# First blocks of the v products: one column piece over two token tiles in place of two pieces over one, with the second tile's rows of x loaded early

## The chip, the cores and the metric

The kernel runs on one core of one Trainium2 chip. The metric is the device time in microseconds of one execution, median of the runs; lower is better. A profiled execution of the kernel, with the start, the length and the waits of each instruction, was taken beside the timed ones.

## What is computed

One step of a two-layer streaming encoder for 1024 prompt rows and 32 sample rows of width 1024 that share all weights. The part that the change touches lies in the first layer:

```python
mod = jax.nn.silu(c) @ w_ada[i] + b_ada[i]
sh1, sc1, gt1, sh2, sc2, gt2 = jnp.split(mod[:, None, :], N_MOD, axis=-1)
h = rmsnorm(x, g_norm[i, 0]) * (1 + sc1) + sh1
...
z = jax.nn.gelu(h @ w_in)
u, v = jnp.split(z, 2, axis=-1)
v = rmsnorm(v, g_v)
vr = v.reshape(bsz, L // T, T, SGU_GROUPS, SGU_GROUP_DIM)
w = w_s[:, :T, :T] * sgu_chunk_mask()[:T, :T].astype(w_s.dtype)
s = jnp.einsum('gij,bnjgd->bnigd', w, vr)
...
return (u * s) @ w_out, v
```

Behind it come a squared-ReLU MLP of width 4096, a second layer with a pooling mixer, and another such MLP. They make up most of the time and are not changed.

## The kernel before

**Tiles and blocks.** The 1056 rows lie in three token tiles of 384, 384 and 288 rows (the last one: 256 prompt rows and the 32 sample rows). For the loads of x and for the v products the rows are cut into nine blocks: 0 to 2 are tile 0, 3 to 5 tile 1, 6 to 8 tile 2, where block 8 has 32 rows. v has 2048 columns, in four column pieces `p` of 512. A product `(p, b)` is the block's 128 rows by the piece's 512 columns, over eight steps `k` of 128 of the inner width. As every fp32 operand is split into a high and a low part (`wh`, `wl` for weights; `hh`, `hl` for activations), each step is three matmuls (`v_mm`, L815 to L832): 24 for a whole product. For block 8 it is two to a step.

**The stream.** All weights and the rows of x are read by DMAs that one list, `stream`, orders (L304 to L337); `issue` (L349) walks along it and starts each load as soon as its buffer allows. There are two kinds of buffer: a ring of three `raw` tiles of 4 KB a partition, used for x, for weights of the products and for the later slices of `w_ada`; and the 16 `W` tiles, which hold the first 16 slices of `w_ada` (those ahead of `first_ada`) and all split weights. All loads are issued by SyncE's queue (SPq), in order, and SPq also issues the stores of v (`v_end`, L844).

**What becomes of an item.** `stream_step` (L541) takes the next item. `do_w` (L369) splits a weight: a copy on ScalarE into `wh` (L372), a subtraction on VectorE into `wl`. `do_x` (L497) squares and sums a block on ScalarE (L502), turns it with eight transposes on TensorE (L512) into two PSUM tiles, which VectorE copies into `acc` (L515). `do_ada_pe` (L394) multiplies an early `w_ada` slice on TensorE (L404); two slices make 256 modulation columns, ScalarE copies them out (L416), TensorE turns them (L421), VectorE folds them (L423) into `mod` and `coef`. Later slices go through VectorE alone (`do_ada`, into `aa`), with a small fold on TensorE (L458).

**The first norm.** `first_norm(t)` (L789) is a generator: `spread` makes the reciprocal roots of a tile's rows (L621 to L641), ending with the small products `pb_h` on TensorE and a copy (L794); then each of eight `next` runs one step k of `apply` (L760): `mt` on VectorE, `hh` on ScalarE (L777), `hl` on VectorE. `h0`, `h1`, `h2` are the three tiles' generators. `hh[t]` and `hl[t]` live in rooms `h` and `l` of tile t, each of 8 x 384 words a partition for tiles 0 and 1.

**The early part** (L857 to L885). Five products run while the modulation still arrives: `(0,0)`, `(0,1)`, `(0,2)`, `(1,0)`, `(1,1)`, all of tile 0, the first three in the PSUM tiles `pd`, the other two in `pu`. Four quarters q follow one another; in each, weight items `v,0,q` and `v,1,q` come in, two steps of `h0` are applied, the next four `w_ada` slices are folded, and each of the five products runs its steps 2q and 2q+1. In quarter 2 the blocks 3 to 5 of x come in and the statistics of tile 1 are made, in quarter 3 the blocks 6 to 8 and those of tile 2. After the last quarter the rest of `h1` and all of `h2` are applied and the five products end (`v_end`: gelu L842, square and sum L843, store L844).

**The order behind it.** `v_order` (L911) lists the remaining products: `(1,2)`, then blocks 3 to 8 of piece 0 and of piece 1, then pieces 2 and 3. After each, `weave` (L612) takes at most one item of the stream. A planner decides whether a later slice of `w_ada` may be taken: it sums its own costs of TensorE (`tick`) and VectorE (`on_dve`) and holds a slice back while VectorE is ahead; the folds of these slices get due times from the same sums. The whole program is then handed to a list scheduler, which fixes for each engine an order of instructions; at run time every engine goes through its list in that order.

Of the kernel before, what the change touches and what calls it, by code (L numbers as in the profile page):

```python
# [16 lines left out]
D = 1024  # L17
# [17 lines left out]
def tile_stream_encoder_step(  # L35
# [33 lines left out]
    def tick(us):  # L69
        time["pe"] += us  # L70
        time["dve"] = max(time["dve"], time["pe"] - 4.0)
# [59 lines left out]
    def room(part, t, name, dtype=F32):  # L131
        return work.tile([P, KB, ncol[t]], dtype, tag=f"h{part}{t}", bufs=1, name=name)
# [13 lines left out]
    def t_c(name):  # L146
        return work.tile([P, 384], F32, tag="c", bufs=3, name=name)
# [7 lines left out]
    def t_raw(name):  # L155
        return work.tile([P, 1024], F32, tag="raw", bufs=RAW_SLOTS, name=name)
# [13 lines left out]
    for i, parts in enumerate(rows):  # L170
        n = sum(k for _, k in parts)
# [11 lines left out]
        v = const.tile([P, n], F32, name=f"vec{i}")  # L183
# [24 lines left out]
    stream = []  # L208
    witem = {}

    def add_w(key, ap, shape):
        stream.append(("w", key, ap, shape))

    def add_ada(l, j):

        sl, q = j // 2, j % 2
        stream.append(
            (
                "ada",
                (l, sl, q),  # L220
                w_ada[l][q * 512 : (q + 1) * 512, sl * 256 : (sl + 1) * 256].rearrange(
                    "(k p) f -> p k f", p=P
                ),
                (4, 256),
            )
        )

    def add_x(b):
        if b < 8:
            ap = x_prompt[0, b * P : (b + 1) * P, :]  # L230
        else:
            ap = x_sample[0]
        stream.append(("x", b, ap, None))

    def v_item(p, q):
        return (
            ("v", p, q),
            sgu_w_in[0][q * 256 : (q + 1) * 256, SGU + p * 512 : SGU + (p + 1) * 512].rearrange(
                "(k p) f -> p k f", p=P
            ),  # L240
            (2, 512),
        )

    def w_vpiece(p):
        for q in range(4):
            add_w(*v_item(p, q))
# [53 lines left out]
    def some_ada(n):  # L300
        for _ in range(min(n, len(rest))):
            add_ada(*rest.pop(0))
# [1 line left out]
    for b in range(3):  # L304
        add_x(b)
    for q in range(4):
        if q == 3:
            for b in range(3, 6):
                add_x(b)
        for j in (8 + 2 * q, 9 + 2 * q, 2 * q, 2 * q + 1):  # L310
            add_ada(0, j)
        for p in range(2):
            add_w(*v_item(p, q))
    first_ada = len(stream)
    for b in range(6, 9):
        add_x(b)
    rest += [(0, j) for j in range(16, 48)]
    some_ada(10)
    for p in range(2, 4):
# [24 lines left out]
    deferred = []  # L344

    def in_raw(k):
        return not (stream[k][0] == "ada" and k < first_ada)

    def issue():  # L349
        while state["issued"] < len(stream):  # L350
            k = state["issued"]
            kind, key, ap, shape = stream[k]
            if in_raw(k):
                if state["raw"] == RAW_SLOTS:
                    return
                state["raw"] += 1
                r = t_raw(f"raw{k}")
            else:
                r = work.tile([P, 1024], F32, tag="W", bufs=W_SLOTS, name=f"raw{k}")
            if kind == "x":  # L360
                nr = P if key < 8 else DEC
                i = nc.sync.dma_start(r[:nr, :], ap)
            else:
                i = nc.sync.dma_start(r.rearrange("p (a b) -> p a b", a=shape[0]), ap)
            raws[k] = r
            loads[key] = i.ins
            state["issued"] += 1
# [122 lines left out]
    def run_deferred(force=False):  # L490
        n = len(deferred)
        while n > 0 and (force or deferred[0][0] <= time["pe"]):
            deferred.pop(0)[1]()
            n -= 1
# [61 lines left out]
    def need_w(key):  # L556
        state["used"] = max(state["used"], wpos[key])
        while key not in witem:
            assert stream_ready(), key
            stream_step()  # L560
        return witem[key]
# [9 lines left out]
    def w_finish(key):  # L571
        wdone.add(key)
# [50 lines left out]
    def spread(t, ss, tag, out, dg):  # L623

        npr, nsm = TILES[t][1], TILES[t][2]
        blk = [(c * P, P) for c in range(npr // P)] + ([(npr, nsm)] if nsm else [])
        nb = len(blk)
        ms, r0, q = t_st(f"ms_{tag}"), t_st(f"r0_{tag}"), t_st(f"q_{tag}")
        ts(ms[:, :nb], ss[:, :nb], 1.0 / D, EPS, op0=ALU.mult, op1=ALU.add)
        act(out=r0[:, :nb], in_=ms[:, :nb], func=AF.Sqrt)  # L630
        nc.vector.reciprocal(out=r0[:, :nb], in_=r0[:, :nb])
        tt(out=q[:, :nb], in0=r0[:, :nb], in1=r0[:, :nb], op=ALU.mult)
        stt(out=q[:, :nb], in0=q[:, :nb], scalar=-0.5, in1=ms[:, :nb], op0=ALU.mult, op1=ALU.mult)
        stt(out=r0[:, :nb], in0=q[:, :nb], scalar=1.5, in1=r0[:, :nb], op0=ALU.add, op1=ALU.mult)
        yield False
        pb = ps_ms(f"pb_{tag}")
        for b, (c0, w) in enumerate(blk):
            act(out=dg[:w, c0 : c0 + w], in_=ident[:w, :w], func=AF.Copy, scale=r0[:w, b : b + 1])
        for b, (c0, w) in enumerate(blk):
            mm(pb[:, c0 : c0 + w], ones[:w, :], dg[:w, c0 : c0 + w], start=True, stop=True)  # L640
        out.append(pb)  # L641
        yield False
# [145 lines left out]
    def first_norm(t):  # L788
        n = ncol[t]  # L789
        nb = 3  # L790
        cp = t_c(f"r_h0_{t}")
        got = []
        yield from spread(t, ssx[:, 3 * t : 3 * t + nb], f"h0_{t}", got, cp)
        act(out=cp[:, :n], in_=got[0][:, :n], func=AF.Copy)  # L794
        yield "statistics"
        yield from apply(t, 0, 0, 0, cp, keep=True)
# [14 lines left out]
    def v_mm(ps, p, b, ks):  # L811
        if b < 8:
            t, c0, m = min(b // 3, 2), (b - 3 * min(b // 3, 2)) * P, P
        else:
            t, c0, m = 2, 256, DEC  # L815
        for k in ks:
            wh, wl = need_w(("v", p, k // 2))
            o = (k % 2) * 512
            if b == 8:
                a = hs[k // 4][:, k % 4, :]  # L820
                tick(0.46)
                mm(ps[: 2 * m, :], a, wh[:, o : o + 512], start=k == 0, stop=False)
                mm(ps[: 2 * m, :], a, wl[:, o : o + 512], start=False, stop=k == KB - 1)
                if k % 2 == 1:
                    w_finish(("v", p, k // 2))
                continue
            tick(0.69)
            a_h = hh[t][:, k, c0 : c0 + m]
            a_l = hl[t][:, k, c0 : c0 + m]
            mm(ps[:m, :], a_h, wh[:, o : o + 512], start=k == 0, stop=False)  # L830
            mm(ps[:m, :], a_h, wl[:, o : o + 512], start=False, stop=False)  # L831
            mm(ps[:m, :], a_l, wh[:, o : o + 512], start=False, stop=k == KB - 1)  # L832
# [13 lines left out]
    def statistics(h):  # L846
        while next(h) != "statistics":
            pass

    def stream_to(kind, key):  # L850
        k = max(i for i, s in enumerate(stream) if s[0] == kind and s[1] == key)
        while state["next"] <= k:
            stream_step()
        run_deferred()


    early = [(0, 0), (0, 1), (0, 2), (1, 0), (1, 1)]  # L857
    early_ps = [(ps_dn if i < 3 else ps_up)(f"pv{p}_{b}") for i, (p, b) in enumerate(early)]
    h0, h1, h2 = (first_norm(t) for t in range(NT))
    stream_to("x", 2)  # L860
    statistics(h0)
    stream_to("ada", (0, 0, 1))
    for q in range(4):
        stream_to("w", ("v", 0, q))
        next(h0)
        stream_to("w", ("v", 1, q))
        next(h0)
        if q < 2:
            stream_to("ada", (0, q + 1, 1))
        elif q == 2:  # L870
            stream_to("x", 5)
            statistics(h1)
            stream_to("ada", (0, 3, 1))
        else:
            stream_to("x", 8)
            statistics(h2)
        for ps, (p, b) in zip(early_ps, early):
            v_mm(ps, p, b, (2 * q, 2 * q + 1))
    for h in (h0, h1):
        for _ in h:  # L880
            pass
    for ps, (p, b) in zip(early_ps, early):
        v_end(ps, p, b)
    for _ in h2:
# [3 lines left out]
    for half in range(2):  # L888
        x = work.tile([P, 384], F32R, tag="rr", bufs=2, name=f"hs{half}")[:, : 8 * DEC].rearrange(
            "p (k n) -> p k n", k=4  # L890
        )
# [16 lines left out]
        stt(out=q, in0=q, scalar=-0.5, in1=m, op0=ALU.mult, op1=ALU.mult)  # L908
        stt(out=x, in0=q, scalar=1.5, in1=x, op0=ALU.add, op1=ALU.mult)

    v_order = [(1, 2)]  # L911
    v_order += [(p, b) for p in range(2) for b in range(3, 9)]
    v_order += [(p, b) for p in range(2, 4) for b in range(9)]
    for p, b in v_order:
        ps = ps_dn(f"pv{p}_{b}")
# [581 lines left out]
```

## Time and profile before

| | us |
|---|---|
| median of 3 runs | 2222.41 (2219.92 to 2223.79) |
| profiled execution, its own time | 2220.61 |
| its span in the trace | 2218.8 |
| TensorE busy in the span | 2187.9 |
| VectorE busy | 1404.1 |
| ScalarE busy | 986.4 |
| mean granted TensorE clock | 0.997 |

Engines are PE (TensorE matmuls), PEld (its weight loads), DVE (VectorE), ACT (ScalarE), POOL (GpSimd) and SP (SyncE); SPq is the DMA issue of SyncE. In a view by instructions in order of time, a row has the start, the duration, the engine and line, the tiles written and read, the count, and in brackets the idle time of the engine before it with what ended it. Matmuls are pipelined: a row's duration is longer than the distance to the next start, and it is the distance that counts. The stretch that the change touches is the first 140 us or so.

### The profile page before, as it was taken

What the parts mean: (1) busy time and instruction counts of PE and PEld (TensorE: products, weight loads), DVE (VectorE), ACT (ScalarE), POOL (GpSimd) and SP (SyncE); (2) the same over time, 40 slices, a digit from 0 to 9 for tenths busy, and PEclk for the clock granted to TensorE, in tenths of its full rate; (3) what the DMA queues carried; (4) which work ended last, traced back from release to release, by engine and by line L of the source; (5) the groups of instructions that cost most, each with busy time, mean ns of one, the idle gap of its engine ahead of it and who ended that gap; (6) DMA issues with size and microseconds to landing.
All of it is one profiled execution on the core that took longest, in us unless ns stands there. A gap on an engine that the chain in (4) does not pass through costs nothing.

```text
span 2218.8 us, 33828 instructions
## 1 busy us (share of the span) xinstructions
PE 2187.9 (99%) x13488; PEld 2096.6 (94%) x13488; DVE 1404.1 (63%) x2646; ACT 986.4 (44%) x1675; POOL 0.7 (0%) x6
## 2 busy tenths in 40 slices
PE   7999999999999999999999999999999999999998
PEld 5777899999999999999999999999999999999998
DVE  4755656665869646676757869878765454433375
ACT  4633423133447553223445556666564542313354
POOL 0000000000000000000000000000000000000000
PEclk9999999999999999999999999999999999999999
DMA  8365533244436543334554556665454552312243
GB/s 299 123 199 196 176 112 126 78 148 126 135 98 194 162 143 124 114 109 125 154 170 140 165 162 187 184 190 155 147 162 140 153 154 64 96 29 77 92 124 110
DMA packets 369090, 312.99 MB, mean 141 GB/s; under 512 B 10818, under 2 KB 345098, under 8 KB 368932
## 3 DMA queue, kind: packets, MB, share of 16 engines
q1 hardware_dynamic: 368660, 310.74, 45.1%
q8 instruction: 105, 1.72, 0.3%
q14 instruction: 53, 0.43, 0.1%
q10 hardware_dynamic: 272, 0.10, 0.0%
HBM read 278.95 MB, written 31.84 MB: 140 GB/s over the span
## 4 chain that ended last, share of the span: by engine, by line
PE 92%; DVE 3%; DMA 3%; ACT 1%; issue 0%; SPq 0%; DVEq 0%; ACTq 0%
PE pf L803 11%; PE pf L804 11%; PE pf L805 11%; PE pg L803 11%; PE pg L804 11%; PE pg L805 11%; PE po L803 3%; PE po L804 3%; PE po L805 3%; PE pu L803 3%; PE pu L805 3%; PE pu L804 3%; PE pv L830 2%; PE pv L831 2%; PE pv L832 2%; DVE aa L79 2%
## 5 line engine op out<-in xcount | busy, mean ns | idle before, releaser
L803 PE MATMUL pg<-fh,wh_dn 128*128 128x384 f32 (+1 forms) x1536 | 499.2, 325 | 0.0
L803 PE MATMUL pf<-hh,wh_up 128*128 128x384 f32 (+1 forms) x1536 | 497.6, 324 | 0.6 <-ACT wh_up L372 0.6
L805 PE MATMUL pf<-hh,wl_up 128*128 128x384 f32 (+1 forms) x1536 | 495.8, 323 | 0.6 <-DVE wl_up L79 0.6
L804 PE MATMUL pf<-hl,wh_up 128*128 128x384 f32 (+1 forms) x1536 | 496.3, 323 | 0.0
L804 PE MATMUL pg<-fl,wh_dn 128*128 128x384 f32 (+1 forms) x1536 | 494.4, 322 | 0.0
L805 PE MATMUL pg<-fh,wl_dn 128*128 128x384 f32 (+1 forms) x1536 | 494.1, 322 | 0.0
L79 DVE TENSOR_TENSOR wl_up<-raw,wh_up 128x1024 fp32r<-128x1024 f32 x152 | 185.8, 1223 | 169.8 <-ACT wh_up L372 169.8
L803 PEld LDWEIGHTS pg<-fh,wh_dn 128*128 128x128 f32 x1536 | 288.5, 188 | 4.0 <-issue 2.4
L803 PEld LDWEIGHTS pf<-hh,wh_up 128*128 128x128 f32 x1536 | 288.2, 188 | 2.8 <-issue 1.4
L804 PEld LDWEIGHTS pg<-fl,wh_dn 128*128 128x128 f32 x1536 | 288.6, 188 | 0.7
L805 PEld LDWEIGHTS pf<-hh,wl_up 128*128 128x128 f32 x1536 | 288.2, 188 | 1.0 <-DVE wl_up L79 1.0
L805 PEld LDWEIGHTS pg<-fh,wl_dn 128*128 128x128 f32 x1536 | 288.6, 188 | 0.0
L804 PEld LDWEIGHTS pf<-hl,wh_up 128*128 128x128 f32 x1536 | 288.2, 188 | 0.4
L372 ACT ACTIVATE wh_up<-raw 128x1024 fp32r<-128x1024 f32 x152 | 161.0, 1059 | 281.5 <-PE pf L804 208.1
L79 DVE TENSOR_TENSOR acc<-acc,pg 128x384 f32<-128x384 f32 (+1 forms) x336 | 173.4, 518 | 141.1 <-PE pg L805 140.5
L372 ACT ACTIVATE wh_dn<-raw 128x1024 fp32r<-128x1024 f32 x152 | 161.0, 1060 | 210.6 <-PE pg L804 164.3
L79 DVE TENSOR_TENSOR wl_dn<-raw,wh_dn 128x1024 fp32r<-128x1024 f32 x152 | 185.9, 1223 | 89.3 <-ACT wh_dn L372 89.0
L79 DVE SCALAR_TENSOR_TENSOR aa<-raw,csil,aa 128x256 f32<-128x256 f32 x560 | 231.2, 478 | 1.8 <-DMA raw<-in_w_ada_dram 1.8
L1121 ACT ACTIVATE r<-pf 128x384 f32<-128x384 f32 (+1 forms) x192 | 86.6, 451 | 202.7 <-PE pf L805 199.3
L79 DVE TENSOR_TENSOR fl<-r,fh 128x384 fp32r<-128x384 f32 (+1 forms) x192 | 100.3, 522 | 105.1 <-ACT fh L957 103.5
L803 PE MATMUL pu<-hh,wh_u 128*128 128x384 f32 (+1 forms) x384 | 126.1, 328 | 0.0
L805 PE MATMUL pu<-hh,wl_u 128*128 128x384 f32 (+1 forms) x384 | 124.4, 324 | 0.8 <-DVE wl_u L79 0.8
(253 smaller groups left out, 2923.7 us busy)
## 6 DMA issues: line engine op xcount, KB each, us to landing
raw<-in_ffn_w_up_dram SPq DMA_DIRECT2D x152, 512.0 KB, 4.1
raw<-in_ffn_w_down_dram SPq DMA_DIRECT2D x152, 512.0 KB, 3.4
raw<-in_w_ada_dram SPq DMA_DIRECT2D x96, 512.0 KB, 4.2
raw<-in_sgu_w_in_dram SPq DMA_DIRECT2D x40, 512.0 KB, 4.1
xd<-acc SPq DMA_DIRECT2D x8, 1536.0 KB, 6.9
raw<-in_sgu_w_out_dram SPq DMA_DIRECT2D x24, 512.0 KB, 3.7
xo_r<-xd SPq DMA_DIRECT2D x32, 384.0 KB, 3.5
vd<-vt SPq DMA_DIRECT2D x32, 256.0 KB, 2.4
```

The source lines that it names most:

```text
L79: return op(out, *args, **kw)
L372: act(out=wh, in_=r, func=AF.Copy)
L803: mm(ps[:, :n], wh, rh, start=i == 0, stop=False)
L804: mm(ps[:, :n], wh, rl, start=False, stop=False)
L805: mm(ps[:, :n], wl, rh, start=False, stop=i == last)
L830: mm(ps[:m, :], a_h, wh[:, o : o + 512], start=k == 0, stop=False)
L831: mm(ps[:m, :], a_h, wl[:, o : o + 512], start=False, stop=False)
L832: mm(ps[:m, :], a_l, wh[:, o : o + 512], start=False, stop=k == KB - 1)
L1121: act(out=r[:, :n], in_=ps[:, :n], func=AF.Relu)
```

## The change

Three things are changed.

- The order of the stream. In each quarter only the item of piece 0 comes in; the four items of piece 1 follow as one run after blocks 6 to 8 of x. Blocks 3 to 5 of x move from quarter 3 of the stream to just behind the first weight item.
- The place of blocks 3 to 5 of x. They are read into the room that `hh[1]` uses afterwards (three blocks of 1024 words fill its 8 x 384 words), and no longer into the ring of three.
- The products of the early part and their order. The five are now blocks 0 to 4 of piece 0; blocks 3 and 4 are of tile 1, so two steps of `h1` are applied in each quarter, after the quarter's products of blocks 0 to 2 and before those of blocks 3 and 4. Blocks 3 to 5 come in and tile 1's statistics are made in quarter 0. Behind the early part the order is `(0,5)`, `(1,0)` to `(1,5)`, then blocks 6 to 8 of both pieces, then pieces 2 and 3 as before.

```diff
     for b in range(3):
         add_x(b)
     for q in range(4):
-        if q == 3:
+        for j in (8 + 2 * q, 9 + 2 * q, 2 * q, 2 * q + 1):
+            add_ada(0, j)
+        add_w(*v_item(0, q))
+        if q == 0:
             for b in range(3, 6):
                 add_x(b)
-        for j in (8 + 2 * q, 9 + 2 * q, 2 * q, 2 * q + 1):
-            add_ada(0, j)
-        for p in range(2):
-            add_w(*v_item(p, q))
     first_ada = len(stream)
     for b in range(6, 9):
         add_x(b)
+    w_vpiece(1)
...
     def in_raw(k):
-        return not (stream[k][0] == "ada" and k < first_ada)
+        return stream[k][1] not in (3, 4, 5) and not (stream[k][0] == "ada" and k < first_ada)
+
+
+    x_rows = room("h", 1, "x_rows").rearrange("p k n -> p (k n)").rearrange("p (b d) -> p b d", d=D)
...
+            elif kind == "x":
+                r = x_rows[:, key - 3, :]
...
-    early = [(0, 0), (0, 1), (0, 2), (1, 0), (1, 1)]
+
+    early = [(0, b) for b in range(5)]
     early_ps = [(ps_dn if i < 3 else ps_up)(f"pv{p}_{b}") for i, (p, b) in enumerate(early)]
     h0, h1, h2 = (first_norm(t) for t in range(NT))
+
+    def early_mm(bs, q):
+        for b in bs:
+            v_mm(early_ps[b], 0, b, (2 * q, 2 * q + 1))
+
     stream_to("x", 2)
     statistics(h0)
     stream_to("ada", (0, 0, 1))
     for q in range(4):
         stream_to("w", ("v", 0, q))
         next(h0)
-        stream_to("w", ("v", 1, q))
         next(h0)
-        if q < 2:
-            stream_to("ada", (0, q + 1, 1))
-        elif q == 2:
+        early_mm((0, 1, 2), q)
+        if q == 0:
             stream_to("x", 5)
             statistics(h1)
-            stream_to("ada", (0, 3, 1))
+        if q < 3:
+            stream_to("ada", (0, q + 1, 1))
         else:
             stream_to("x", 8)
             statistics(h2)
-        for ps, (p, b) in zip(early_ps, early):
-            v_mm(ps, p, b, (2 * q, 2 * q + 1))
-    for h in (h0, h1):
-        for _ in h:
-            pass
+        next(h1)
+        next(h1)
+        early_mm((3, 4), q)
     for ps, (p, b) in zip(early_ps, early):
         v_end(ps, p, b)
...
-    v_order = [(1, 2)]
-    v_order += [(p, b) for p in range(2) for b in range(3, 9)]
+    v_order = [(0, 5)]
+    v_order += [(1, b) for b in range(6)] + [(p, b) for p in range(2) for b in range(6, 9)]
     v_order += [(p, b) for p in range(2, 4) for b in range(9)]
```

## The prediction

> **What bounds the kernel now.** I read the page's first part, then the busy times by stretch, then TensorE's groups and its instructions in order of time for the stretch that the change touches, last the queue of SyncE and the groups of VectorE and ScalarE.
>
> ```profile
> span 2218.8 us, 33828 instructions
> PE 2187.9 (99%) x13488; PEld 2096.6 (94%) x13488; DVE 1404.1 (63%) x2646; ACT 986.4 (44%) x1675; POOL 0.7 (0%) x6
> ```
>
> TensorE is busy nearly throughout; 2218.8 - 2187.9 = 30.9 us are all that it idles, so an edit that adds and removes no matmul can save no more than a part of that. The change ends before 141 us, so the next view splits the first 154 us at the first v product, at the end of the five early ones, and at the start of piece 2. Columns: stretch, its length, PE, PEld, DVE and ACT busy with instruction counts, POOL, granted clock, DMA share, GB/s.
>
> ```profile
> 16.00:24.20 8.20, 6.85 (x58) 2.92 (x58) 2.62 (x9) 3.63 (x9) 0.00 (x0) 0.79 1.03 339
> 24.20:69.60 45.40, 43.42 (x266) 30.66 (x266) 31.50 (x73) 26.77 (x47) 0.00 (x0) 1.00 0.77 258
> 69.60:141.00 71.40, 71.31 (x334) 55.12 (x335) 42.19 (x117) 31.90 (x78) 0.00 (x0) 1.00 0.35 116
> 141.00:154.20 13.20, 10.19 (x41) 6.60 (x39) 8.25 (x16) 5.10 (x7) 0.00 (x0) 0.87 0.72 234
> ```
>
> The early part shows 45.40 - 43.42 = 2.0 us of idle TensorE, the stretch behind it 0.1 us. But busy is not peak, so I work out what the early part's instructions need back to back. Their groups, and the rows from which the distances between starts come (two rows of 128 x 512 products with 31 starts between them, a run of 16 modulation products, a run of 16 transposes, each with the row that follows it):
>
> ```profile
> L830 PE MATMUL pv<-wh_v,hh 128*128 128x512 f32 x40 | 16.2, 417 | 0.1
> L831 PE MATMUL pv<-wl_v,hh 128*128 128x512 f32 x40 | 16.1, 403 | 0.0
> L832 PE MATMUL pv<-wh_v,hl 128*128 128x512 f32 x40 | 15.9, 398 | 0.0
> L404 PE MATMUL ada<-raw,csil 128*32 128x256 f32 x80 | 6.6, 388 | 1.6 <-DMA raw<-in_w_ada_dram 1.6
> L512 PE MATMUL xT<-ident,raw 128*128 128x128 f32 x40 | 5.2, 274 | 0.0
> L421 PE MATMUL adat<-ident,adas 128*128 128x128 f32 x12 | 2.3, 276 | 0.0
> L640 PE MATMUL pb_h<-r_h,ones 128*128 128x128 f32 x6 | 1.3, 320 | 0.0
> L512 PE MATMUL xT<-ident,raw 32*128 32x32 f32 x8 | 0.7, 224 | 0.0
> ```
>
> ```profile
> 23.08 1.07 PE L404 MATMUL ada<-raw,csil 128*32 128x256 f32 x16
> 24.26 0.96 PE L830 MATMUL pv<-wh_v,hh 128*128 128x512 f32 x3
> ...
> 45.37 2.04 PE L512 MATMUL xT<-ident,raw 128*128 128x128 f32 x16
> 47.16 0.48 PE L830 MATMUL pv<-wh_v,hh 128*128 128x512 f32 x1
> ...
> 55.55 1.07 PE L404 MATMUL ada<-raw,csil 128*32 128x256 f32 x16
> 56.55 0.50 PE L830 MATMUL pv<-wh_v,hh 128*128 128x512 f32 x1
> ...
> 69.69 0.50 PE L830 MATMUL pv<-wh_v,hh 128*128 128x512 f32 x1 [0.42 <-ACT pv L843]
> ...
> 73.56 0.39 PE L830 MATMUL pv<-wh_v,hh 128*128 128x512 f32 x1
> ...
> 80.66 0.39 PE L831 MATMUL pv<-wl_v,hh 128*128 128x512 f32 x1
> ```
>
> A product matmul takes (80.66 - 73.56)/31 = 0.229 us, a modulation product 1.00/16 = 0.063, a transpose 1.79/16 = 0.112. So: 120 x 0.229 = 27.5, 80 x 0.063 = 5.0, 40 x 0.112 = 4.5, and for the last small groups at most their busy 2.3 + 1.3 + 0.7 = 4.3: 41.3 us of 45.4. The early part is **bound by TensorE** with 4 us of holes, 2.0 us of them named: 1.6 for modulation slices still in transit, and 0.42 at 69.69, where `(1,2)` waits for the PSUM tile of `(0,0)`.
>
> **The change part by part.** Nothing is computed more or less often: 36 v products, 16 early slices, nine blocks of x and 16 splits remain. What moves is when.
>
> *Transit of the slices (-1.6).* The rows of SPq show why the slices of quarter 2 were late:
>
> ```profile
> 15.59 9.66 SPq L364 DMA_DIRECT2D raw<-in_sgu_w_in_dram  x2
> 25.31 2.29 SPq L364 DMA_DIRECT2D raw<-in_w_ada_dram  x4
> ```
>
> The second of these weight loads stands at the queue's head for most of 9.66 us until a ring tile comes free, and the four slices queue behind it until 25.31. In the new order the item of piece 1 is gone and blocks 3 to 5 need no ring tile, so up to the third weight item SPq waits only for tiles that x held. Twenty transfers stand up to the end of quarter 2's slices (x 6, slices 12, weights 2); at 524 KB and the 339 GB/s of the stretch before 24.2 each takes 1.55 us, so the last lands at about 32 us, before TensorE, with blocks 3 to 5 and ten more products ahead of it, asks. The wait goes whole. 2 MB less travel ahead of quarter 3; that part was already hidden.
>
> *End of the first three products (-0.4).* Blocks 0 to 2 finish twelve matmuls (2.7 us) ahead of 3 and 4, so their gelus can run before `(0,5)` needs a tile.
>
> *Transposes of blocks 3 to 5 (-1.0).* 24 x 0.112 = 2.7 us leave the bound stretch, if they fit ahead of 24.26, where TensorE does 6.85 of 8.20 us at a granted clock of 0.79; the 16 modulation products at 23.08 (1.07) fall behind in exchange, as their slices now land three transfers later. Bounds: -1.6 (all fit) and 0 (none). I take -1.0, since the data of block 3 can land only after seven transfers and one weight item, about 8 x 1.55 + 2 = 14 us, which leaves most of the stretch.
>
> *What blocks 3 to 5 add ahead of the first products (+0.5).* ScalarE gets three squares, VectorE six copies, ahead of or between tile 0's steps:
>
> ```profile
> L515 DVE COPY acc<-xT 128x512 f32<-128x512 f32 x6 | 3.8, 685 | 3.1 <-PE xT L512 3.1
> L79 DVE TENSOR_TENSOR wl_v<-raw,wh_v 128x1024 fp32r<-128x1024 f32 x8 | 9.7, 1223 | 0.7 <-ACT wh_v L372 0.6
> L79 DVE SCALAR_TENSOR_TENSOR mt<-acc,coef,r_h 128x384 f32<-128x384 f32 x8 | 4.7, 616 | 0.1
> L79 DVE SCALAR_TENSOR_TENSOR hl<-mt,mod,hh 128x384 fp32r<-128x384 f32 x6 | 3.4, 613 | 0.7 <-ACT hh L777 0.7
> ```
>
> VectorE is busy 2.62 of 8.20 us before 24.2, so there is room; only a copy standing in its order ahead of tile 0's first `mt` costs. Bounds 0 and 2.0 (three copies); I take 0.5.
>
> *Tile 1's steps inside the quarters (+0.2).* Two steps are 2 x (616 + 613) = 2.5 us of VectorE. A quarter then has 2.5 + 2.5 + 1.2 for one split and about 1 for the folds: 7.2 us, beside at least 30 x 0.229 + 32 x 0.063 = 8.9 us of TensorE; it keeps up. In quarter 0 the copies and the statistics come on top (3.8 + 1), 12 us beside 8.9 + 2.7: TensorE may stand for tile 1's `hh` before blocks 3 and 4. Bounds 0 and 1.5; in its queue the products of blocks 0 to 2 stand ahead, so 0.2. The rest of `h1`, 16 x 0.61 = 10 us, leaves the time after the early part.
>
> *Piece 1's splits (+0.5).* Before, they were done during the quarters. Now `(0,5)`, 24 x 0.229 = 5.5 us, is all that covers them, at about 67.5 to 73 us, and they share VectorE and ScalarE with the steps of tile 2 and the ends of five products:
>
> ```profile
> L79 DVE SCALAR_TENSOR_TENSOR aa<-raw,csil,aa 128x256 f32<-128x256 f32 x14 | 6.1, 475 | 0.0
> L79 DVE SCALAR_TENSOR_TENSOR hl<-mt,mod,hh 128x256 fp32r<-128x256 f32 x8 | 3.8, 480 | 0.3 <-ACT hh L777 0.3
> L79 DVE SCALAR_TENSOR_TENSOR mt<-acc,coef,r_h 128x256 f32<-128x256 f32 x8 | 3.8, 479 | 0.0
> L79 DVE SCALAR_TENSOR_TENSOR mt<-acc,coef,r_h 128x32 f32<-128x32 f32 x8 | 2.0, 247 | 0.0
> L79 DVE SCALAR_TENSOR_TENSOR hl<-mt,mod,hh 128x32 fp32r<-128x32 f32 x8 | 2.0, 247 | 0.1
> ...
> raw<-in_sgu_w_in_dram SPq DMA_DIRECT2D x40, 512.0 KB, 4.1
> ```
>
> Tile 2's steps are 3.8 + 3.8 + 2.0 + 2.0 = 11.6 us of VectorE, the four splits 4 x 1.22 = 4.9. In this same stretch the 14 `aa` instructions (6.1 us), later in the program than those steps, ran between them; the splits can do so as well, and the 10 us of tile 1's steps are gone. Bounds: 0, and 7.5 us if every step of tile 2 goes first (rival 2). Nearest to the `aa` row, I take 0.5.
>
> *Behind it (0).* By the planner's own sums both versions reach the same state after the twelfth product behind the early part, and the folds of the later slices follow the 6th, 8th, 10th and 12th in both. The hole at the start of piece 2 (13.20 - 10.19 = 3.0 us) therefore moves along.
>
> **Sum:** -1.6 - 0.4 - 1.0 + 0.5 + 0.2 + 0.5 = -1.8 us. The profiled execution took 2220.61 (1.8 around its span); it becomes 2218.8. The median lies 1.8 us above it: **2220.6**.
>
> A wait put in newly may cost more than its length:
>
> ```profile
> 144.05 0.48 PE L458 MATMUL ada<-aa,pick 128*32 128x128 f32 x4 [2.27 <-DVE aa L79]
> ```
>
> Behind this idle 2.27 us lies the low clock of the last stretch: (1 - 0.87) x 13.20 = 1.7 us lost. The Trainium skill (TensorE: Matmul & The Clock Gate, Part 1) states half rate after an idle window of about 3.4 us, which would spare a wait as short as this; the trace shows the loss after 2.27 us, and the trace decides. By that rule rival 2 would cost 1.7 us less.
>
> **Rivals.**
>
> *1. All holes go: faster.* The 4 us of holes close, not just the named 2.0, and the transposes give their 1.6: -5.6, 2216.8. For it: more independent products are ready at every point. Against: some of the holes are changes between kinds of matmul, which stay.
>
> *2. Piece 1 is late: slower.* VectorE takes tile 2's steps first. The last copies of x end near 63 us, the statistics take 3, the steps 11.6, the first split 1.2: 79, when TensorE has stood at `(1,0)` since 73, so about 5.2 to 6. The fourth item needs the ring tile that the first split frees: 4.1 to land, 1.1 for `wh` and 1.2 for `wl` are 6.4 us beside 18 x 0.229 = 4.1 of products: 2.3 more. With 1.7 of low clock, 9.2 to 10, less the 2.3 net gained before: +7, 2229.4. It decides once the first `wl` comes over 4 us after the end of `(0,5)`. For it: these steps are earlier in the program. Against: the `aa` row.
>
> *3. The loads were hidden anyway.* TensorE bounds the part, and small waits for tile 1 replace those removed: 0, 2222.4.
>
> **How the numbers follow.** About 0.2% (4.4 us) is what a measurement of this kernel can tell from no change. Forecast 0.33 (own range 2218 to 2223), rival 3 0.18, rival 1 0.22, rival 2, whole or in part above +4.4, 0.22; 0.05 for blocks 3 to 5 holding up tile 0 by more than 5 us. So same 0.51, faster 0.22, slower 0.27. The range reaches to rival 1's value and most of the way to rival 2's: 2216.5 to 2227.5.
>
> **What would show it.** Right: no idle of TensorE on `in_w_ada_dram` after 24 us; transposes of blocks 3 to 5 before 26; the first product after the early part at 67 to 68.5; less than 1 us of waiting for `wl_v` or `wh_v` at `(1,0)`; the 2.27 us wait found again, some 2 us earlier. Wrong: a wait for `hh` in quarters 0 or 1, the first product later than 25.5, or one of several us for `wl_v` between 70 and 85.

## The result: slower by 0.34%, and the profile after

| | before | changed |
|---|---|---|
| median, us | 2222.84 (2219.92 to 2224.61, 6 runs) | 2229.76 (2228.87 to 2232.67, 6 runs) |
| ratio, with its 95% interval | | 1.0034 (1.0021 to 1.0047) |
| profiled execution's span, us | 2218.8 | 2227.7 |

The forecast was 2220.6 with a range to 2227.5, so the time lies outside it. It lies within 0.4 us of the second rival's 2229.4, but by another way, as the rows show. The medians lie 6.9 us apart, the two profiled executions that are read below 8.9 us by their spans.

The page's first part for the changed kernel: the busy time of TensorE is 3.4 us longer than before, its idle time in the span 2227.7 - 2191.3 = 36.4 us where it was 30.9.

```profile
span 2227.7 us, 33816 instructions
PE 2191.3 (98%) x13488; PEld 2101.1 (94%) x13488; DVE 1404.0 (63%) x2646; ACT 984.9 (44%) x1673; POOL 0.7 (0%) x6
```

Busy times by stretch, the same stretches and columns as in the prediction:

```profile
16.00:24.20 8.20, 6.99 (x44) 3.23 (x45) 1.80 (x7) 5.05 (x12) 0.00 (x0) 0.60 1.06 370
24.20:69.60 45.40, 37.08 (x241) 26.34 (x240) 26.60 (x64) 19.27 (x37) 0.00 (x0) 0.96 0.55 175
69.60:141.00 71.40, 71.40 (x336) 55.77 (x335) 44.25 (x119) 33.31 (x77) 0.00 (x0) 1.00 0.48 151
```

The loss is in the second row: TensorE idles 45.40 - 37.08 = 8.3 us where it idled 2.0, and the granted clock is 0.96 where it was 1.00. In the third row it does not idle at all. A mark far behind is the last `adat` fold of the run of pieces 0 and 1, one single row, at 141.04 us before and here:

```profile
148.94 0.27 PE L479 MATMUL adat<-ident,adas 128*128 128x128 f32 x1
...
151.94 0.41 PE L463 MATMUL ada<-aa,pick 128*32 128x128 f32 x4 [2.26 <-DVE aa L79]
```

So 148.94 - 141.04 = 7.9 of the span's 8.9 us are lost before this point. They are made of 8.3 - 2.0 = 6.3 us of idle time and at most (1.00 - 0.96) x 45.40 = 1.8 and (0.79 - 0.60) x 8.20 = 1.6 us of low clock; that is 9.7, an upper bound, because low clock while TensorE idles costs nothing.

TensorE in order of time, the rows in which it waited or changed its work:

```profile
23.87 3.61 PE L517 MATMUL xT<-ident,x_rows 128*128 128x128 f32 x24
...
31.22 1.60 PE L645 MATMUL pb_h<-r_h,ones 128*128 128x128 f32 x6 [3.74 <-ACT r_h L643]
...
39.97 0.44 PE L426 MATMUL adat<-ident,adas 128*128 128x128 f32 x2 [1.40 <-ACT adas L421]
...
44.50 1.44 PE L835 MATMUL pv<-wh_v,hh 128*128 128x512 f32 x5 [1.09 <-ACT wh_v L377]
```

The first v product starts at 44.50 us; before, it started at 24.26. For 20 us TensorE has only slices, folds, transposes and the small statistics products; where one of them waits for ScalarE, as in the rows above, there is no product to fill the gap. ScalarE shows what the first product waited for:

```profile
43.41 1.04 ACT L377 ACTIVATE wh_v<-raw 128x1024 fp32r<-128x1024 f32 x1
...
44.86 2.00 ACT L377 ACTIVATE wh_v<-raw 128x1024 fp32r<-128x1024 f32 x2
```

and SyncE's queue, when the weight had been asked for:

```profile
10.90 0.37 SPq L369 DMA_DIRECT2D raw<-in_sgu_w_in_dram  x1
11.32 1.42 SPq L367 DMA_DIRECT2D x_rows<-in_x_prompt_dram  x3
12.78 5.32 SPq L369 DMA_DIRECT2D raw<-in_w_ada_dram  x4
...
27.90 5.55 SPq L369 DMA_DIRECT2D raw<-in_w_ada_dram  x4
```

The load was issued at 10.90 us, and the last four of the sixteen slices by 27.90 + 5.55 = 33.45; yet the weight's high part `wh_v` was copied at 43.41, with the next two weights' copies right behind it. Nothing ends a wait of ScalarE in the 43.41 row: the copy was neither late in its data nor slow, it **stood late in ScalarE's order**. In the kernel before the same copy began at 22.55 us:

```profile
22.55 1.05 ACT L372 ACTIVATE wh_v<-raw 128x1024 fp32r<-128x1024 f32 x1
```

### The profile page after: what moved, and what is told of

Its sections match the earlier page's. It is cut to its first block, busy times and chain, and to the rows that moved or that the text cites. A ratio compares the mean times of both kernels' runs of the same rounds, so it can differ in the third digit from the quotient of the medians.

```text
span 2227.7 us, 33816 instructions
## 1 busy us (share of the span) xinstructions
PE 2191.3 (98%) x13488; PEld 2101.1 (94%) x13488; DVE 1404.0 (63%) x2646; ACT 984.9 (44%) x1673; POOL 0.7 (0%) x6
## 4 chain that ended last, share of the span: by engine, by line
PE 92%; DVE 3%; DMA 2%; ACT 1%; issue 0%; DVEq 0%; SPq 0%; ACTq 0%
PE pf L808 11%; PE pf L810 11%; PE pf L809 11%; PE pg L808 11%; PE pg L809 10%; PE pg L810 10%; PE po L808 3%; PE po L809 3%; PE po L810 3%; PE pv L836 3%; PE pv L835 3%; PE pv L837 3%; PE pu L808 2%; PE pu L810 2%; PE pu L809 2%; DVE aa L79 2%
```

## The experiments

**The theories.** In the kernel before, the ring of three `raw` tiles stopped `issue` early: eight of the first sixteen `w_ada` slices stood in the program ahead of the first split. In the changed kernel blocks 3 to 5 need no ring tile and a quarter has one weight item, so `issue` runs through and all sixteen slices' loads stand ahead of it. Slices and split weights share the 16 `W` tiles.

- *Theory A*: what counts is the order in which the program asks for these tiles. The list scheduler keeps the order of the writers of one pool, so the first split comes into its order only behind the load of the last slice that the program has put ahead of it, and what ScalarE and TensorE could do until then goes first.
- *Theory B*: the 16 tiles are simply full, and the split waits for one to come free.
- *Theory C*: blocks 3 to 5 and tile 1's statistics and steps, which now come first, fill the engines.

All kernels compute the whole reference. The times stand beside the kernel before in the same series, whose medians were 2224.23 us (28 runs) for hold_23, hold_123, spare_tiles and x_in_ring, 2223.97 (21 runs) for room_alone and hold_and_shift, and 2221.11 (15 runs) for room_and_hold and shift_alone.

### Slices held back: hold_23 and hold_123

The changed kernel, in which `issue` stops ahead of an early slice until an earlier weight item has been split (hold_23; in hold_123 the last two lines are `q >= 1` and `q - 1`):

```diff
             k = state["issued"]
             kind, key, ap, shape = stream[k]
+            if kind == "ada" and k < first_ada:
+                q = sum(it[0] == "w" for it in stream[:k])
+                if q >= 2 and ("v", 0, q - 2) not in witem:
+                    return
```

> The changed kernel, with the slices of w_ada of quarter 2 asked for only after the first weight item is split, those of quarter 3 after the second. Theory A (order of asking): the split tiles of the first weight item are asked for behind all sixteen slices, which the new stream lets through at once, so its copy to wh is ordered late and the first product starts at 44.5 us; here it must start by 30 us, and the time comes to 2218 to 2224 us. Theory B (tiles run out: sixteen slices fill the sixteen W tiles): the same here. Theory C (blocks 3 to 5, tile 1's statistics and steps stand in front of the products): the first product stays later than 40 us and the time at 2227 to 2232.

> The changed kernel, with the slices of each quarter after the first asked for only after the weight item of the quarter before is split. Theory A: the copy to wh is ordered earlier still; first product by 27 us, 2216 to 2223 us. Theory B: as in the run that holds quarters 2 and 3. Theory C: first product after 40 us, 2227 to 2232.

hold_23: 2226.71 us (2223.45 to 2228.72), ratio 1.0010 (1.0001 to 1.0019). hold_123: 2224.47 us (2222.78 to 2228.26), ratio 1.0003 (0.9994 to 1.0011). Both first products came as early as Theory A had them (26.57 and 25.62 us), but both times lie above the ranges that had been given for it, by 2.7 and 1.5 us (the kernel before, too, ran 1.4 us slower in this series than in that of the result), and hold_23 stays slightly slower than the kernel before. The early part of hold_123, first its busy times, then its first split and first product in order of time:

```profile
24.20:69.60 45.40, 41.65 (x271) 29.62 (x270) 30.39 (x73) 22.95 (x44) 0.00 (x0) 1.00 0.57 187
```

```profile
16.53 1.04 ACT L381 ACTIVATE wh_v<-raw 128x1024 fp32r<-128x1024 f32 x1
...
25.62 0.50 PE L839 MATMUL pv<-wh_v,hh 128*128 128x512 f32 x1
```

With the split ahead of the slices the copy begins at 16.53 instead of 43.41, the first product 19 us earlier, and in hold_123 no loss in time can be told any more, though TensorE still idles 3.75 us where the kernel before idled 2.0. Its waits in this stretch are of another kind than before:

```profile
PE adat L430 <- ACT adas L425: 2.9, 5, 0.8
PE pv L839 <- ACT hh L786: 0.8, 2, 0.4
```

The columns are the sum, the count and the longest. These are waits for the folds of the slices; before, no such wait came after 24.20 us.

### Two W tiles left free: spare_tiles

The changed kernel, in which the last two of the sixteen slices are read into room `h` of tile 2, so that two `W` tiles are never taken by slices; the order of the loads stays.

```diff
+    spare = [k for k, it in enumerate(stream) if it[0] == "ada" and k < first_ada][-2:]
+    h2_rows = room("h", 2, "h2_rows").rearrange("p k n -> p (k n)")[:, :2048].rearrange("p (b d) -> p b d", d=D)
...
+            elif k in spare:
+                r = h2_rows[:, spare.index(k), :]
```

> The changed kernel, with the last two of the sixteen early slices read into the room of tile 2's hh, so that two W tiles are free when the first weight item is split; the order of asking is kept. Theory A: the split is still asked for behind fourteen slices; the first product starts after 35 us, 2224 to 2231 us. Theory B: it starts by 28 us, 2217 to 2224 us. Theory C: after 40 us, 2227 to 2232.

2231.82 us (2229.79 to 2233.40), ratio 1.0029 (1.0017 to 1.0041). The first split had two tiles free and yet came at 40.12 us, the first product at 41.63:

```profile
40.12 1.05 ACT L382 ACTIVATE wh_v<-raw 128x1024 fp32r<-128x1024 f32 x1
...
41.63 1.44 PE L840 MATMUL pv<-wh_v,hh 128*128 128x512 f32 x5
```

Theory B falls: it is not the number of tiles. That the split came 3 us earlier fits A, since fourteen slices, no longer sixteen, ask for `W` tiles ahead of it. The time lies 0.8 us above A's range and, like the first product after 40 us, within what C had been given: this run alone does not tell A from C.

### The blocks through the ring: x_in_ring

The changed kernel with blocks 3 to 5 read through the ring again; order of the stream and the products stay as changed.

```diff
-        return stream[k][1] not in (3, 4, 5) and not (stream[k][0] == "ada" and k < first_ada)
+        return not (stream[k][0] == "ada" and k < first_ada)
```

> The changed kernel, with blocks 3 to 5 of x read through the ring of three as in the kernel before, in their new place of the stream. Theory A: the ring stops the stream ahead of quarter 1's slices, so the first split is early (wh before 20 us) and no product waits for it, but what follows comes later: the second split again stands behind the later slices; first product by 28 us, 2221 to 2230 us. Theory B: as A for the first product. Theory C: first product after 40 us.

2226.07 us (2223.40 to 2230.04), ratio 1.0009 (1.0000 to 1.0017). ScalarE and TensorE:

```profile
16.88 1.06 ACT L377 ACTIVATE wh_v<-raw 128x1024 fp32r<-128x1024 f32 x1 [0.20 <-DMA raw<-in_sgu_w_in_dram]
...
42.89 1.04 ACT L377 ACTIVATE wh_v<-raw 128x1024 fp32r<-128x1024 f32 x1
...
24.17 0.51 PE L835 MATMUL pv<-wh_v,hh 128*128 128x512 f32 x1
```

The full ring now stops the stream, the first split comes at 16.88 and the first product at 24.17, with the same products and steps in the same program order. So those do not push the first product back: Theory C falls for the first product. Only the first split is saved; the second one still stands at 42.89 us, behind the slices that ran ahead once the ring had room.

### The room alone, without and with the hold: room_alone and room_and_hold

The other half of the change by itself: the kernel before, with blocks 3 to 5 early and in their own room, but with its own five products and two weight items a quarter. room_and_hold adds the hold of hold_123 to it.

```diff
-        if q == 3:
-            for b in range(3, 6):
-                add_x(b)
...
         for p in range(2):
             add_w(*v_item(p, q))
+        if q == 0:
+            for b in range(3, 6):
+                add_x(b)
...
-        if q < 2:
-            stream_to("ada", (0, q + 1, 1))
-        elif q == 2:
+        if q == 0:
             stream_to("x", 5)
             statistics(h1)
...
+        if q < 3:
+            stream_to("ada", (0, q + 1, 1))
```

> Blocks 3 to 5 of x go early into their own room, as in the changed kernel, but the five early products and the weight items of two pieces per quarter stay as before. Theory A (the loss comes from tiles of the stream asked for ahead of the first split; here two weight items per quarter fill the ring and stop the stream): first v product at 24 to 27 us, TensorE busy over 41 of 45.4 us between 24.2 and 69.6, time 2220 to 2226. Theory C (blocks 3 to 5 and tile 1's statistics ahead of the first product are themselves the loss): the first product after 35 us and the time above 2227.

> room_alone plus the hold: slices of quarter 1 and later are asked for only once the first weight item of the quarter before is split; the order of the loads, the own room for blocks 3 to 5 and the five products stay. If room_alone lost its 5 us to the late asking (in it the first copy wh_v began at 27.46 us, behind the three squares of x_rows, although its load was issued at 10.99): wh_v begins before 22.5, the first v product before 26.5, and the time is 2221 to 2225. If the three squares, 24 transposes and the statistics of tile 1 are themselves the loss, wherever the split stands: the first product may come earlier, but the time stays at 2227.5 or more.

room_alone: 2229.36 us (2225.94 to 2231.05), ratio 1.0021 (1.0012 to 1.0030). This missed what Theory A had been given: the first product came at 28.56, not by 27, and the time lies above 2226. Its time is the one that C gave, though C's first product after 35 us was wrong too. ScalarE ahead of the first split:

```profile
23.53 1.05 ACT L506 ACTIVATE xsq<-x_rows 128x1024 f32<-128x1024 f32 x1
...
25.39 1.12 ACT L781 ACTIVATE hh<-mt,mod 128x384 fp32r<-128x384 f32 x2 [0.73 <-DVE mod L79]
26.43 1.04 ACT L506 ACTIVATE xsq<-x_rows 128x1024 f32<-128x1024 f32 x1
...
27.46 1.04 ACT L376 ACTIVATE wh_v<-raw 128x1024 fp32r<-128x1024 f32 x1
```

Either the squares are the load (C), or the split stands behind them because it is asked for late (A). The hold tells them apart, because it leaves the squares where they are: room_and_hold took 2220.39 us (2219.32 to 2223.71), ratio 0.9999 (0.9990 to 1.0007), slightly below the 2221 to 2225 that had been given. The two kernels in the early stretch, first room_alone:

```profile
24.20:69.60 45.40, 40.43 (x253) 26.38 (x251) 29.80 (x64) 23.10 (x42) 0.00 (x0) 0.96 0.68 220
```

then room_and_hold, its busy times, and in order of time its first split, and the last of its squares with the second split behind it:

```profile
24.20:69.60 45.40, 44.20 (x279) 30.80 (x280) 34.55 (x79) 28.10 (x50) 0.00 (x0) 1.00 0.76 251
```

```profile
16.61 1.06 ACT L380 ACTIVATE wh_v<-raw 128x1024 fp32r<-128x1024 f32 x1
...
25.15 1.04 ACT L510 ACTIVATE xsq<-x_rows 128x1024 f32<-128x1024 f32 x1
...
26.19 1.05 ACT L380 ACTIVATE wh_v<-raw 128x1024 fp32r<-128x1024 f32 x1
```

With the same squares and the split asked for ahead of the slices no loss is left, and TensorE idles 1.2 us, less than before. C falls as the cause of the loss. The kernel before was not run with the hold alone, so a small cost of the squares that the hold makes good is not ruled out.

In room_alone, though, the split is not late because more slices ask first. By the program (`issue` and the order of its calls) two weight items a quarter still stop at the ring, and eight slices stand ahead of the first split, as in the kernel before. What changed is when the last of them is loaded: the second four now stand behind the three loads of blocks 3 to 5 in SyncE's queue. First the kernel before, then room_alone:

```profile
13.34 2.14 SPq L364 DMA_DIRECT2D raw<-in_w_ada_dram  x4
```

```profile
14.54 5.22 SPq L368 DMA_DIRECT2D raw<-in_w_ada_dram  x4
```

They are issued by 13.34 + 2.14 = 15.48 and by 14.54 + 5.22 = 19.76 us, 4.3 us apart; the first splits are 27.46 - 22.55 = 4.9 us apart.

### One quarter later, without and with the hold: shift_alone and hold_and_shift

The changed kernel with blocks 3 to 5, tile 1's statistics and steps one quarter later, and the products of blocks 3 and 4 by one weight item behind those of blocks 0 to 2. hold_and_shift has the hold of hold_123 besides.

```diff
         add_w(*v_item(0, q))
-        if q == 0:
+        if q == 1:
             for b in range(3, 6):
                 add_x(b)
...
-        if q == 0:
+        if q == 1:
             stream_to("x", 5)
             statistics(h1)
+            next(h1)
+            next(h1)
         if q < 3:
             stream_to("ada", (0, q + 1, 1))
...
-        next(h1)
-        next(h1)
-        early_mm((3, 4), q)
+        if q:
+            early_mm((3, 4), q - 1)
+            next(h1)
+            next(h1)
+    early_mm((3, 4), 3)
```

> As hold_123 (slices of quarter q asked for only once weight item q-1 is split), and blocks 3 to 5, tile 1's statistics and the products of blocks 3 and 4 come one quarter later, so that products of an earlier item are at hand while a quarter's slices are folded. If the rest of the loss in hold_123 (TensorE idle 3.75 us between 24.2 and 69.6, 4.5 of it in waits for adas at a window one us wider) is want of ready products: those waits fall below 3 us, TensorE is busy over 42.5 of 45.4 us, and the time is 2220 to 2223.5, at or below before. If the folds are late of themselves (transit or ScalarE), the waits for adas stay at 4 to 5 us and the time at 2224 to 2227.

> hold_and_shift without its hold: blocks 3 to 5, tile 1's statistics and the products of blocks 3 and 4 one quarter later, but the slices are asked for freely, as in the changed kernel. If the asking is what counts: the first copy wh_v stands behind the folds of quarters 1 and 2 again, the first v product comes at 36 to 46 us, and the time is 2227 to 2232. If the place of blocks 3 to 5 was the cause: the first product comes at 24 to 28 us and the time at 2222 to 2225.

shift_alone: 2233.37 us (2227.84 to 2237.06, 5 runs), ratio 1.0049 (1.0036 to 1.0063), the highest ratio of all, though its interval overlaps that of the changed kernel; its time lies 1.4 us above the range given for late asking, and its first product came at 48.43 us, later than the 46 that was given. The profiled execution is the slowest of its five (2237.06 us). hold_and_shift: 2222.81 us (2221.29 to 2226.55), ratio 0.9993 (0.9984 to 1.0002), as expected. First shift_alone, its busy times and its first product, then hold_and_shift, its busy times and TensorE's waits from 24 to 70 us:

```profile
24.20:69.60 45.40, 37.17 (x216) 24.86 (x213) 24.19 (x59) 21.79 (x40) 0.00 (x0) 0.84 0.52 168
```

```profile
48.43 1.92 PE L835 MATMUL pv<-wh_v,hh 128*128 128x512 f32 x4 [2.52 <-ACT wh_v L377]
```

```profile
24.20:69.60 45.40, 43.45 (x283) 31.00 (x283) 32.67 (x84) 28.85 (x60) 0.00 (x0) 0.99 0.64 210
```

```profile
PE adat L430 <- ACT adas L425: 1.1, 2, 0.6
PE adat L430 <- DMA raw<-in_w_ada_dram: 0.5, 1, 0.5
PE pv L839 <- ACT hh L786: 0.2, 1, 0.2
```

So the place of blocks 3 to 5 does not cure it, the hold does. And with products of an earlier item at hand, the waits for the folds go from hold_123's 2.9 us to 1.1 (the 4.5 us that the expectation names count from 16 us on): much of what was left in hold_123 was want of ready products. In time the two are not told apart, as their intervals overlap.

### All together

| kernel | ratio to before (95%) | early slices ahead of the first split | last of them issued by, us | first split, us | first product, us | TensorE idle, 24.2 to 69.6 |
|---|---|---|---|---|---|---|
| before | 1 | 8 | 15.48 | 22.55 | 24.26 | 2.0 |
| changed | 1.0034 (1.0021 to 1.0047) | 16 | 33.45 | 43.41 | 44.50 | 8.3 |
| hold_23 | 1.0010 (1.0001 to 1.0019) | 8 | 18.03 | 25.48 | 26.57 | 4.2 |
| hold_123 | 1.0003 (0.9994 to 1.0011) | 4 | 7.77 | 16.53 | 25.62 | 3.8 |
| spare_tiles | 1.0029 (1.0017 to 1.0041) | 14 in `W` tiles | 32.08 | 40.12 | 41.63 | 7.4 |
| x_in_ring | 1.0009 (1.0000 to 1.0017) | 4 | 7.83 | 16.88 | 24.17 | 4.1 |
| room_alone | 1.0021 (1.0012 to 1.0030) | 8 | 19.76 | 27.46 | 28.56 | 5.0 |
| room_and_hold | 0.9999 (0.9990 to 1.0007) | 4 | 7.55 | 16.61 | 24.79 | 1.2 |
| shift_alone | 1.0049 (1.0036 to 1.0063) | 16 | 33.24 | 47.34 | 48.43 | 8.2 |
| hold_and_shift | 0.9993 (0.9984 to 1.0002) | 4 | 7.78 | 16.80 | 25.25 | 2.0 |

The third column is read from the program, the fourth from SyncE's queue. In the six kernels with eight slices or more ahead, the first split begins 7.1 to 14.1 us behind the issue of the last of them; in the four with four ahead it begins at 16.5 to 16.9 us.

As differences of these ratios the hold alone is worth 0.31, 0.22 and 0.56% in three pairs; the two kernels of a pair stood in different series, each beside the kernel before, so each difference carries both intervals. No version is faster than the kernel before by more than its interval.

## Why the prediction was wrong, by its own steps

**The step that failed** is "What blocks 3 to 5 add ahead of the first products (+0.5)", with its bounds 0 and 2.0 and the sentence "only a copy standing in its order ahead of tile 0's first `mt` costs". It counted the squares and copies themselves. With the hold they and the early loads cost nothing that can be told in time (room_and_hold). What was overlooked is that blocks 3 to 5 and the items of piece 1, by leaving the ring together, took away the stop that had kept the slices of quarters 2 and 3 behind the first split in the program: 16 slices stand ahead of it, no longer 8 (8 with the blocks alone out of the ring, 4 with the items alone). The prediction used the same fact on its gain side, in the step on transit ("up to the third weight item SPq waits only for tiles that x held"), and did not ask what else stood in the order behind those loads. The bound of 2.0 us was far too small: the first product came 44.50 - 24.26 = 20.2 us later, which the prediction itself had named as a sign of being wrong ("the first product later than 25.5"). The step measured, with its low clock, most of the 7.9 us at 148.94, and 0.31% of the time, about 6.9 us, by the difference to hold_123. The chance of 0.05 for "blocks 3 to 5 holding up tile 0 by more than 5 us" was the nearest case to what happened, and far too small.

**Transit of the slices (-1.6): right.** TensorE has no wait on `in_w_ada_dram` after 24 us in the changed kernel. There this proves little, since TensorE came late to the slices; but hold_123, whose first product starts at 25.62, has none either. The gain could not be seen, because idle time of another cause took its place.

**Transposes of blocks 3 to 5 (-1.0): not gained in the changed kernel.** They begin at 23.87 us, before 26 as given, but run to 23.87 + 3.61 = 27.48, so nearly all of them lie behind 24.26, inside the stretch that they were to leave. In room_and_hold 16 of the 24 do come ahead of the first product, at 22.69. It ends pieces 0 and 1 earlier than the kernel before by 141.04 - 139.45 = 1.6 us, which the transposes and the transit share in a way that no run tells:

```profile
139.45 0.27 PE L482 MATMUL adat<-ident,adas 128*128 128x128 f32 x1
```

Its span is shorter by 0.9 us only (2217.9), and the ratio 0.9999 does not tell it from nothing.

**Tile 1's steps inside the quarters (+0.2): too small.** In hold_123, which has the changed products without the late split, TensorE waits 0.8 us for `hh` and 2.9 us for folds. This is close to rival 3's "small waits for tile 1 replace those removed", though most of it is for folds, and its ratio of 1.0003 is rival 3's result. With the slices held, rival 3 would have been the nearest case.

**Piece 1's splits (+0.5) and rival 2: did not occur.** From 69.60 to 141.00 TensorE is busy 71.40 of 71.40 us; no wait for `wl_v` or `wh_v` at `(1,0)`. That is not only because everything came later there: hold_123 has 71.40 of 71.40 as well. In the changed kernel the first split of piece 1 comes at 70.57 us, ahead of tile 2's steps, whose first `hh` stands at 79.10; the other three, from 83.24 to 88.07, come between those steps, as the prediction had read from the `aa` row:

```profile
70.57 1.06 ACT L377 ACTIVATE wh_v<-raw 128x1024 fp32r<-128x1024 f32 x1 [2.00 <-DMA raw<-in_sgu_w_in_dram]
```

That the time met rival 2's figure is chance.

**Behind it (0): right.** The wait at the start of piece 2, 2.27 us at 144.05 before, is found again as 2.26 at 151.94, moved by the same 7.9 us as the mark ahead of it. The prediction had it some 2 us earlier, not later. The last 1.0 us of the span's 8.9 arises later: from 208.81 to 212.22 us the changed kernel has a granted clock of 0.50, which is worth at most 1.7 us and which the kernel before does not have there. Other kernels have such a stretch too (room_and_hold at 198.13), so it does not come from the late split; no run was made for it.

**End of the first three products (-0.4): right in kind.** The changed kernel has no wait of this kind, but its first three products also ended much later. hold_123 and hold_and_shift, where they did not, have none from 24 to 150 us either; 0.4 us is too little to tell in the time.

What stays open: that the hold cures the late split is shown; that the scheduler does it by keeping the order of a pool's writers is argued, from which kernels have an early split and which do not, and from how the first split follows the load of the last slice ahead of it in the table. A kernel that keeps the loads ahead and takes the split weights from a pool of their own wasn't tried.

## What to carry to other kernels

A buffer that is full does two jobs: it delays loads, and it keeps later requests in the program behind earlier uses; before a transfer is given a buffer of its own, list which requests now run ahead in the program and who asks for tiles of the same pool behind them, and which loads now stand behind it in the queue. Where loads run ahead freely, stop them by an explicit condition on the consumer that must come first; in three pairs this condition alone decided between a loss of 0.2 to 0.5% and none. And when one engine is busy 99%, the first thing to look for after a reorder is the start of its main work (24.26 to 44.50 us here), not the length of the waits that the change was about.

## What the runs showed of the hardware that was not expected

TensorE ran at half clock for long though it was mostly busy. In shift_alone four stretches of 3.40 us in a row, the first and the last of them shown (columns as in the busy times by stretch; the granted clock is the third number from the end):

```profile
17.60:21.00 3.40, 2.90 (x23) 1.11 (x21) 0.00 (x0) 0.88 (x2) 0.00 (x0) 0.55 1.10 351
...
27.80:31.20 3.40, 2.90 (x23) 1.80 (x13) 1.59 (x6) 0.85 (x2) 0.00 (x0) 0.50 1.09 348
```

TensorE is busy 2.90 of 3.40 us, 85%, by instructions that the low clock itself has lengthened.

So through a stretch without dense products the clock can stay low, which makes it longer; this may be part of why shift_alone has the highest ratio. The busy share does not tell when the low clock ends: in the kernel before TensorE was busy 2.93 of 3.41 us from 17.97 to 21.38 at a clock of 0.50, and the clock was 1.00 behind it.

The other surprise is what starts the low clock. In the changed kernel TensorE waits 1.74 us before this row, and the clock of the stretch from 16.00 is 0.60; in x_in_ring it waits 2.09 us at the same place, and the clock of that stretch stays at 1.00:

```profile
16.21 0.49 PE L645 MATMUL pb_h<-r_h,ones 128*128 128x128 f32 x2 [1.74 <-ACT r_h L643]
```

```profile
16.14 0.49 PE L645 MATMUL pb_h<-r_h,ones 128*128 128x128 f32 x2 [2.09 <-ACT r_h L643]
```

```profile
16.00:24.20 8.20, 6.45 (x59) 3.94 (x59) 4.61 (x12) 5.68 (x13) 0.00 (x0) 1.00 0.90 308
```

The Trainium skill (TensorE: Matmul & The Clock Gate, Part 1) states half rate after at least one idle window of about 3.4 us. The wait of 3.74 us that ends at 31.22 agrees with it: no TensorE instruction from 27.80 to 31.20, then 0.52 in the next 3.40 us. The two rows above do not: the shorter wait was followed by the low clock, the longer one was not.

```profile
27.80:31.20 3.40, 0.00 (x0) 0.00 (x0) 2.56 (x9) 0.63 (x3) 0.00 (x0) 1.00 1.09 348
31.20:34.60 3.40, 3.38 (x22) 1.90 (x22) 0.00 (x0) 1.05 (x3) 0.00 (x0) 0.52 1.07 361
```

Length alone does not decide. The traces' records of the granted clock show what else does: in all ten kernels every stretch of one clock between two changes is a whole multiple of 3.413 us long, so the clock changes only on a grid of that step, which begins at another time in each execution. Cut along its own grid, the changed kernel has the whole wait of 1.74 us (14.47 to 16.21) in one step; x_in_ring's 2.09 us (14.05 to 16.14) lie across the border at 15.35. First the changed kernel, then x_in_ring:

```profile
14.25:17.66 3.41, 1.67 (x10) 0.92 (x8) 1.26 (x5) 0.99 (x3) 0.00 (x0) 1.00 1.04 404
17.66:21.07 3.41, 2.92 (x23) 1.02 (x25) 0.01 (x1) 1.67 (x3) 0.00 (x0) 0.50 1.05 374
```

```profile
11.94:15.35 3.41, 1.91 (x12) 1.26 (x12) 3.29 (x8) 0.61 (x2) 0.00 (x0) 1.00 1.09 372
15.35:18.77 3.42, 2.63 (x22) 1.36 (x22) 1.01 (x3) 2.46 (x5) 0.00 (x0) 1.00 1.03 390
```

Over the first 235 us of the ten traces, from the first record of the clock on, the 20 steps at full clock in which TensorE was busy 1.58 us or less were all followed by the low clock, and none of the 577 with 2.0 us or more was; the 16 steps between these values went either way. hold_123 has a wait of 2.09 us too (14.00 to 16.09), all but the last 0.02 us of it in its step from 12.66 to 16.07: TensorE was busy 1.34 us there, and the clock behind it was 0.50. So a wait far shorter than a step can start the low clock if it falls into one step, and one as long can pass if a border cuts it.
